# A decoder layer on one core: splits of the first pair's DMA sums queued behind the input's turned half, turns two ahead of products, first logistic functions at the end

## The chip, the core and the metric

The kernel runs on one core of one Trainium2 chip. The time is the device time of one execution in microseconds (us). TensorE (PE in the profile) does the matrix products, PEld its weight loads, VectorE (DVE) and ScalarE (ACT) the elementwise work, GpSimd (POOL) elementwise work and the issue of summing DMAs, SyncE (SP) the issue of the other DMAs.

## What is computed

One inference step of a hybrid decoder layer: a prompt of 1024 rows and 64 sample rows (8 x 8), 1024 wide, go through a root-mean-square norm, one wide input projection (seven slices of 512 columns and three gates of 1024), three branches and a gated merge.

```
def layer(x, ...):
    h = rmsnorm(x, g_pre)
    proj = h @ w_in                        # 1024 x (7*512 + 3*1024)
    p_in, p_gate, c_val, c_glu, c_gate, q, x_gate = slices of 512
    a     = pool_mix(p_in) * silu(p_gate)
    u     = c_val * sigmoid(c_glu)         # then depthwise conv 31, layernorm, silu
    bconv = conv_branch(u) * silu(c_gate)
    cattn = attention(q, mem_kv(mem)) * silu(x_gate)
    merged = sum over 3 of sigmoid(merge_logits) * (branch @ w_branch)
    return x + rmsnorm(merged @ w_out, g_post)
```

## The kernel before, in words

Everything is float32 outside; a product is made of float16 halves. `hilo` (line 74) splits a tile: ScalarE writes the high half (line 75), VectorE or, where asked, GpSimd the rest (lines 77 and 79). `mm3` (line 81) makes one product of three matmuls (lines 85, 88, 89): high by high, high by low, low by high.

The input projection goes by pairs of 128 output columns. `pair` (line 446) makes a 2 x 2 block product with seven products instead of eight: the left factors are blocks of the weight and their sums s1 to s4, the right ones are blocks of the turned (transposed) input, B11, B21, B22, and differences T1 to T4. The input's factors are made once, at the start, and kept in `BO`; those of the weight are made for every pair. The weight's sums are DMAs that add into the loaded tile: ScalarE negates two blocks (line 498), GpSimd issues the four sums one after the other (lines 499, 505, 506, 507), each after the landing of the one before. Then the sums are split as the other blocks are. The first `pair` of the list (the value half of the convolution's gate) is begun early: its product of a11 and of a12 are made in the start (`early`).

`startup` (line 236) is a generator. It norms and turns the first half of the input (512 rows: B11, B21), makes the first product with it for two blocks of gate columns (`first`, tiles `sg0`), takes the logistic function of each with its eviction (line 280), then turns the second half. `second_half(k)` (line 290), for k from 0 to 3, turns two blocks, each into a PSUM bank of the kind pb (4 banks), and makes of them by VectorE (lines 292 and 295) two differences `tq`, and by `hilo` the block B12, the block B22 and T1. T2 to T4 follow from `tq`: T3 and T4 are differences that GpSimd makes (lines 312 and 313), T4's low half too. The second half of the gate columns is then made with B12 and B22, and the sample rows (`BS`) follow. `mem_kv` (line 336) scales the 256 memory rows, whose norm's root was begun in the start (line 272).

The program is written in one order, but a scheduler that simulates the timeline places the instructions of each engine; each engine then runs its queue in order. Program order sets who is preferred: in the start the first product of the second gate block stands between `second_half(0)` and `second_half(1)`, and the splits of the pair's sums (lines 475 to 478, tiles `ws`) may go anywhere that their data allow.

Of the kernel before, what the change touches and what calls it, by code (L numbers as in the profile page):

```python
# [9 lines left out]
ALU = mybir.AluOpType  # L11
# [35 lines left out]
def hybrid_layer_kernel(ctx, tc, i, o):  # L47
# [23 lines left out]
    def tiny(shape, dt=F32):  # L71
        return sb.tile(shape, dt, tag="tiny", bufs=24, name=nm("t"))
# [80 lines left out]
        nc.vector.scalar_tensor_tensor(r, r, sc, t, ALU.mult, ALU.mult)  # L153
        return r

    def rstd_of(ss, inv_n, sc=1.0):
        p, n = ss.shape
        s = tiny([P, n])[:p]
        nc.scalar.activation(s, ss, AF.Sqrt, scale=inv_n, bias=eps[:p])
        v = tiny([P, n])[:p]  # L160
        nc.vector.tensor_scalar(v, ss, inv_n, EPS, ALU.mult, ALU.add)
        return newton(s, v, (p, n), sc)
# [3 lines left out]
        (eng or nc.sync).dma_start(out=x[:rows], in_=src)  # L166
        return x[:rows]

    def rstds(xs):
        ss = tiny([P, len(xs)])[: xs[0].shape[0]]  # L170
        for t, x in enumerate(xs):
            nc.scalar.activation(junk[: x.shape[0]], x, AF.Square, accum_out=ss[:, t : t + 1])
        return rstd_of(ss, 1.0 / D)

    BO = cst.tile([P, 7, 2, 4, HALF], F16, name="BO")
    junk = BO[:, 6].rearrange("p a k n -> p (a k n)")[:, : 2 * D].bitcast(F32)
# [59 lines left out]
    def startup():  # L236
# [32 lines left out]
                rs_.append(rstds(xt[k + 1 - k // 4 * 2 : k + 3 - k // 4 * 2]))  # L269

        xs_r = rstds([xs])
        mem["r"] = rstds(mems)
        sg0.update({r: Q([P, T]) for r in range(2)})

        def first(r, t0, ops):
            p = pm()
            for kh in range(2):
                w, n = w0[2 * kh + r], ops[kh]
                mm3(p, [(w[:, 0, k, :], w[:, 1, k, :], n(k)[0], n(k)[1]) for k in range(4)], kh == 0, kh == 1)
            nc.scalar.activation(sg0[r][:, t0 : t0 + HALF], p, AF.Sigmoid, scale=1.0 / WS)  # L280

        first(0, 0, [lambda k: bo(B11, k), lambda k: bo(B21, k)])
        scale_x(xt[4:6], rs_[0], True)
# [6 lines left out]
        def second_half(k):  # L290
            p, gk = flip(k, 1)
            nc.vector.scalar_tensor_tensor(tq[k][:, 0], p, gk, hx[k][:, 0], ALU.mult, ALU.subtract)
            hilo(p, b12[k // 2][:, 0, k % 2], b12[k // 2][:, 1, k % 2], gk)
            p, gk = flip(k + 4, 1)
            nc.vector.scalar_tensor_tensor(tq[k][:, 1], p, gk, tq[k][:, 0], ALU.mult, ALU.subtract)
            hilo(p, *bo(B22, k), gk)
            hilo(tq[k][:, 0], *bo(T1, k), -1.0)

        second_half(0)
        yield  # L300
        first(1, 0, [lambda k: bo(B11, k), lambda k: bo(B21, k)])
        yield
        for k in range(1, 4):
            second_half(k)
            yield
        for k in range(4):
            hilo(tq[k][:, 1], *bo(T2, k), -1.0)
        for r in range(2):
# [19 lines left out]
        for r in range(2):  # L328
            for kh in range(2):
                w = w0[2 * kh + r]  # L330
                mm3(p[:, r * NS : (r + 1) * NS], [(w[:, 0, k, :], w[:, 1, k, :], BS[:, 0, 4 * kh + k, :], BS[:, 1, 4 * kh + k, :]) for k in range(4)], kh == 0, kh == 1)
            nc.scalar.activation(sg0[r][:, S:], p[:, r * NS : (r + 1) * NS], AF.Sigmoid, scale=1.0 / WS)

    def mem_kv():
        memT = [Q([P, 2, KT // 2, NMEM], F16) for _ in range(2)]
        for t, m in enumerate(mems):
            nc.vector.tensor_scalar(m, m, mem["r"][:, t : t + 1], None, ALU.mult)

# [62 lines left out]
    def states():  # L403
        stc = Q([120, 2, W])
        nc.sync.dma_start(
            out=stc, in_=i["state_conv"][0].rearrange("b r c -> (b r) c").rearrange("(a p) c -> p a c", p=120))
        stp = Q([120, W])
        nc.sync.dma_start(out=stp, in_=i["state_pool"][0].rearrange("b r c -> (b r) c"))
        pwr = Q([P, WT, P])
        nc.sync.dma_start(out=pwr, in_=i["pool_w"][0].rearrange("g c d -> c g d"))  # L410
        yield
        for ch in range(WT):
            p = pb()
            for a in range(2):
                nc.tensor.transpose(p[:, a * 120 : (a + 1) * 120], stc[:, a, ch * P : (ch + 1) * P], ident[:120, :120])
            nc.scalar.activation(us[:, ch, :, :CB], p[:, :240].rearrange("p (b j) -> p b j", b=DB), AF.Copy)
            if ch % 2:
                yield
        p = pb()
        for g in range(WT):  # L420
            nc.tensor.transpose(p[:, g * 120 : (g + 1) * 120], stp[:, g * P : (g + 1) * P], ident[:120, :120])
        nc.scalar.activation(es[:, :, :, :PB], p[:, :480].rearrange("p (g b j) -> p g b j", g=WT, b=DB), AF.Copy)
        nc.gpsimd.memset(corr, 1.0)
        for g, win in enumerate(WINS):
            for j in range(win - 1):
                nc.gpsimd.memset(corr[:, g, j : j + 1], float(win) / (j + 1))
        hilo(pwr, pws[:, 0], pws[:, 1], WS)
        yield
        nc.sync.dma_start(out=o["conv_s"][0][:, : CB - DS, :], in_=i["state_conv"][0][:, DS:, :])
        nc.sync.dma_start(out=o["pool_s"][0][:, : PB - DS, :], in_=i["state_pool"][0][:, DS:, :])  # L430
        yield
# [14 lines left out]
    def pair(c0, dest, block, smp, sc=1.0 / WS):  # L446
# [26 lines left out]
                prep_a11()  # L473

        def prep1():
            spl("s1", lambda: v["s1"])
        def prep2():
            spl("s2", lambda: v["s2"])
        def prep3():
            spl("a12", lambda: A(0, 1))  # L480

# [930 lines left out]
```

## Time and profile before

| | us |
|---|---|
| median of 3 runs | 921.75 (921.71 to 926.39) |
| profiled execution | 925.56 |
| its span, first to last instruction | 923.8 |
| mean granted clock of TensorE | 0.965 |
| busy: PE / DVE / ACT / POOL | 859.6 / 715.1 / 465.2 / 360.3 |

A row of a timeline gives the start, the duration, the engine, the line, the operation and its tiles (out<-in, buffer numbers left out), the count of like instructions merged in the row, and in brackets the idle time of the engine ahead of it and what ended it. A row of stages gives start:end, the length, the busy time of each engine with its count of instructions, the granted clock of TensorE (1.00 is full), the share of DMA and GB/s. A row of groups gives count, busy us, mean ns, and idle time before.

### The profile page before, as it was taken

How to read it: one execution, taken by the hardware profiler on the slowest of the kernel's cores; microseconds unless marked ns; L12 is line 12 of the kernel's file. 1: busy time of each engine (PE TensorE's matmuls, PEld its weight loads, DVE VectorE, ACT ScalarE, POOL GpSimd, SP SyncE). 2: the span in 40 equal slices, each digit the busy share in tenths (PEclk: the TensorE clock that was granted, in tenths of full speed). 3: DMA queues.
4: the chain of work that ended last, by engine and by line, in shares of the span. 5: the costliest groups of instructions: out<-in, count | busy, mean ns of one | idle time of the engine just before them, and what ended most of it. 6: DMA issues, size and time to landing. Idle time of an engine off the chain costs nothing.

```text
span 923.8 us, 15244 instructions
## 1 busy us (share of the span) xinstructions
PE 859.6 (93%) x5765; PEld 461.0 (50%) x5765; DVE 715.1 (77%) x1119; ACT 465.2 (50%) x990; POOL 360.3 (39%) x392
## 2 busy tenths in 40 slices
PE   5879999999999889999998989999999999988986
PEld 3325455554555545555444445565545555545432
DVE  4697599999967699999988978458565544678876
ACT  8766547554753733323444544356345434745541
POOL 1354152444343361311443775525355212366500
PEclk8869999999999899999999999999999999998998
DMA  8634742424466224334444336444654658472132
GB/s 300 158 65 144 210 97 56 82 68 113 106 224 176 92 39 102 82 80 92 93 95 92 80 86 123 113 110 97 139 117 105 138 122 251 101 158 60 69 126 91
DMA packets 101541, 107.43 MB, mean 116 GB/s; under 512 B 5486, under 2 KB 72036, under 8 KB 101452
## 3 DMA queue, kind: packets, MB, share of 16 engines
q1 hardware_dynamic: 82748, 68.24, 23.5%
q0 software_dynamic: 18720, 38.22, 23.1%
q8 instruction: 45, 0.74, 0.3%
q14 instruction: 28, 0.23, 0.1%
HBM read 62.37 MB, written 6.33 MB: 74 GB/s over the span
## 4 chain that ended last, share of the span: by engine, by line
PE 37%; DVE 15%; issue 5%; ACT 3%; POOL 3%; DMA 3%; DVEq 0%; ACTq 0%; POOLq 0%
PE pm L85 8%; PE pm L89 8%; PE pm L88 8%; DVE q L715 6%; PE pb L85 4%; PE pb L89 4%; PE pb L88 4%; DVE ws L79 3%; DMA raw<-raw 2%; DVE ws L77 1%; POOL sr L594 1%; ACT ws L75 1%; DVE q L1272 1%; DVE q L1265 1%; DVE q L1155 1%
## 5 line engine op out<-in xcount | busy, mean ns | idle before, releaser
L85 PE MATMUL pm<-BO,ws 128*128 128x512 f16 x836 | 319.9, 385 | 17.8 <-ACT h L513 3.7
L89 PE MATMUL pm<-BO,ws 128*128 128x512 f16 x836 | 320.8, 384 | 3.1 <-DVE ws L77 2.8
L88 PE MATMUL pm<-BO,ws 128*128 128x512 f16 x836 | 321.1, 384 | 1.1 <-DVE BO L77 0.6
L79 DVE SCALAR_TENSOR_TENSOR ws<-raw,ws 128x512 f16<-128x512 f32 x228 | 192.9, 863 | 61.2 <-ACT ws L75 59.5
L88 PEld LDWEIGHTS <-ws 128*128 128x128 f16 x1548 | 149.1, 99 | 134.8 <-issue 27.7
L89 PEld LDWEIGHTS <-ws 128*128 128x128 f16 x1548 | 149.3, 99 | 125.0 <-issue 8.0
L85 PEld LDWEIGHTS <-ws 128*128 128x128 f16 x1548 | 148.7, 99 | 117.7 <-issue 9.5
L75 ACT ACTIVATE ws<-raw 128x512 f16<-128x512 f32 x228 | 138.1, 627 | 119.5 <-PE pm L89 57.0
L715 DVE SCALAR_TENSOR_TENSOR q<-q,cw,q 128x1024 f32<-128x1024 f32 x120 | 166.9, 1399 | 4.3 <-ACT q L712 4.0
L85 PE MATMUL pb<-q,ws 128*128 128x364 f16 (+1 forms) x288 | 92.2, 323 | 2.1 <-DVE q L1155 2.1
L89 PE MATMUL pb<-q,ws 128*128 128x364 f16 (+1 forms) x288 | 93.0, 323 | 0.0
L88 PE MATMUL pb<-q,ws 128*128 128x364 f16 (+1 forms) x288 | 92.9, 323 | 0.0
L499 POOL DMA_DIRECT2D raw<-raw x25 | 21.8, 872 | 150.3 <-ACT raw L498 134.1
L513 ACT ACTIVATE h<-pm 128x512 f32<-128x512 f32 x75 | 44.0, 588 | 50.8 <-PE pm L89 47.2
L1155 DVE SCALAR_TENSOR_TENSOR q<-pb,q 128x364 f32<-128x364 f32 (+1 forms) x72 | 37.1, 528 | 30.0 <-PE pb L89 24.4
L466 DVE SCALAR_TENSOR_TENSOR q<-pm,h 128x512 f32<-128x512 f32 x51 | 34.9, 684 | 21.3 <-PE pm L89 13.3
L507 POOL DMA_DIRECT2D raw<-raw x25 | 22.1, 885 | 68.5 <-issue 24.3
L75 ACT ACTIVATE q<-q 128x1024 f16<-128x1024 f32 (+2 forms) x37 | 35.5, 971 | 26.5 <-DVE q L867 12.6
L506 POOL DMA_DIRECT2D raw<-raw x25 | 21.6, 864 | 64.6 <-DVE ws L79 24.7
L498 ACT ACTIVATE raw<-raw 128x512 f32<-128x512 f32 x50 | 31.0, 626 | 30.7 <-DVE ws L79 29.9
L85 PE MATMUL pm<-BS,ws 128*128 128x64 f16 x416 | 43.3, 193 | 1.2 <-DVE q L466 1.2
L664 ACT ACTIVATE q<-q 128x512 f32<-128x512 f32 x36 | 22.6, 627 | 41.7 <-DVE q L466 41.2
(245 smaller groups left out, 1335.1 us busy)
## 6 DMA issues: line engine op xcount, KB each, us to landing
raw<-in_w_in SPq DMA_DIRECT2D x104, 256.0 KB, 2.9
raw<-raw POOLq DMA_DIRECT2D x104, 256.0 KB, 3.2
q<-in_x_prompt SPq DMA_DIRECT2D x16, 512.0 KB, 9.1
q<-q POOLq DMA_DIRECT2D x14, 544.0 KB, 5.5
raw<-in_w_branch SPq DMA_DIRECT2D x24, 256.0 KB, 3.9
q<-in_w_mem_kv SPq DMA_DIRECT2D x8, 512.0 KB, 6.7
q<-in_cache_mem_k SPq DMA_DIRECT2D x8, 512.0 KB, 3.4
q<-in_cache_mem_v SPq DMA_DIRECT2D x8, 512.0 KB, 7.3
```

Of the source, the lines that this page charges most:

```text
L75: nc.scalar.activation(hi, src, AF.Copy, scale=scale)
L79: nc.vector.scalar_tensor_tensor(lo, src, scale, hi, ALU.mult, ALU.subtract)
L85: ins = nc.tensor.matmul(out, wh, xh, start=start and j == 0, stop=False, skip_group_check=partial)
L88: nc.tensor.matmul(out, wh, xl, start=False, stop=False, skip_group_check=partial)
L89: nc.tensor.matmul(out, wl, xh, start=False, stop=stop and j == n - 1, skip_group_check=partial)
L466: nc.vector.scalar_tensor_tensor(dst, ps, sc, base, ALU.mult, ALU.add)
L498: nc.scalar.activation(A(1, kh), A(1, kh), AF.Copy, scale=-1.0)
L507: nc.gpsimd.dma_start(out=A(0, 1), in_=A(0, 0), accum_op=ALU.add)
L513: nc.scalar.activation(v[name], ps, AF.Copy, scale=sc)
L664: nc.scalar.activation(dst, src, AF.Sigmoid, scale=scale)
L715: ins = nc.vector.scalar_tensor_tensor(acc, src, wj, acc, ALU.mult, ALU.add)
L1155: nc.vector.scalar_tensor_tensor(g, p, 1.0 / WS, g, ALU.mult, ALU.mult)
```

## The change

- The splits of s1 and s2 of the first pair, the end of the memory rows' norm and the split of the pooling weight are put in the queues of ScalarE and VectorE behind the last split of T1 (`second_half(3)`), by `queued()`. The scheduler may not place them ahead of it.
- `second_half(1)` now stands ahead of the second gate block's first product, and `second_half(2)` right behind it.
- The logistic function is no longer taken with each eviction of `sg0`: these are copies now, and at the end of the start one logistic function over each whole tile (1088 columns) follows.
- The memory rows' squares and root stay in the start; the reciprocal root is made in `mem_kv`.

```diff
+    behind = []
+    def queued():
+        es_ = contextlib.ExitStack()
+        for ins in behind:
+            es_.enter_context(tc.issue_after(ins.ins))
+        return es_
...
-        mem["r"] = rstds(mems)
+        mem["ss"] = squares(mems)
+        mem["s"] = root_of(mem["ss"], 1.0 / D)
...
-            nc.scalar.activation(sg0[r][:, t0 : t0 + HALF], p, AF.Sigmoid, scale=1.0 / WS)
+            nc.scalar.activation(sg0[r][:, t0 : t0 + HALF], p, AF.Copy, scale=1.0 / WS)
...
-            hilo(tq[k][:, 0], *bo(T1, k), -1.0)
+            hi, lo = bo(T1, k)
+            a = nc.scalar.activation(hi, tq[k][:, 0], AF.Copy, scale=-1.0)
+            return a, nc.vector.scalar_tensor_tensor(lo, tq[k][:, 0], -1.0, hi, ALU.mult, ALU.subtract)
         second_half(0)
         yield
+        second_half(1)
+        yield
         first(1, 0, [lambda k: bo(B11, k), lambda k: bo(B21, k)])
+        second_half(2)
         yield
-        for k in range(1, 4):
-            second_half(k)
-            yield
+        behind.extend(second_half(3))
+        yield
...
-            nc.scalar.activation(sg0[r][:, S:], p[:, r * NS : (r + 1) * NS], AF.Sigmoid, scale=1.0 / WS)
+            nc.scalar.activation(sg0[r][:, S:], p[:, r * NS : (r + 1) * NS], AF.Copy, scale=1.0 / WS)
+            nc.scalar.activation(sg0[r], sg0[r], AF.Sigmoid)
...
     def mem_kv():
+        with queued():
+            mem["r"] = rstd_of(mem["ss"], 1.0 / D, s=mem["s"])
...
-        hilo(pwr, pws[:, 0], pws[:, 1], WS)
+        with queued():
+            hilo(pwr, pws[:, 0], pws[:, 1], WS)
...
         def prep1():
-            spl("s1", lambda: v["s1"])
+            with queued() if ahead else contextlib.nullcontext():
+                spl("s1", lambda: v["s1"])
         def prep2():
-            spl("s2", lambda: v["s2"])
+            with queued() if ahead else contextlib.nullcontext():
+                spl("s2", lambda: v["s2"])
```

How the queues change is read from the instructions of each engine in their new order. The lines of the changed file are some other lines: L77, L79 and L81 there are L75, L77 and L79 of before, L301 and L313, L316 are L280 and L292, L295, L319 and L320 the two halves of T1, L337 and L338 are L312 and L313, L530 to L538 are L499 to L507, L544 is L513, L161 and L169 are L159 and L161, L180 is L172.

ScalarE before, from the last square of the memory rows on (`raw_126` holds the first pair's s1, `raw_642` and `raw_645` the second pair's weights, `pb` a turned block, `q_328` a difference):

```order
L172 ACTIVATE BO,t_276<-q_106 128x1024
L75 ACTIVATE ws_648<-raw_126 128x512
L75 ACTIVATE ws_651<-raw_642 128x512
L75 ACTIVATE ws_654<-raw_645 128x512
L280 ACT_TABLE_LOAD
L280 ACTIVATE q_290<-pm_292 128x512
L159 ACT_TABLE_LOAD
L159 ACTIVATE t_279<-t_276,eps 128x2
L498 ACTIVATE raw_642<-raw_642 128x512
L498 ACTIVATE raw_645<-raw_645 128x512
L75 ACTIVATE q_326<-pb_332,g_pre 128x512
L75 ACTIVATE BO<-q_328 128x512
```

The same place in the changed kernel (`pb_323` is block 0's first turn, `pb_341` block 1's, `h_489` a difference that GpSimd makes):

```order
L180 ACTIVATE BO,t_276<-q_106 128x1024
L301 ACTIVATE q_281<-pm_283 128x512
L161 ACTIVATE t_279<-t_276,eps 128x2
L544 ACTIVATE h_375<-pm_362 128x512
L77 ACTIVATE q_317<-pb_323,g_pre 128x512
L319 ACTIVATE BO<-q_319 128x512
L77 ACTIVATE BO<-pb_331,g_pre 128x512
L77 ACTIVATE BO<-q_319 128x512
L77 ACTIVATE q_317<-pb_341,g_pre 128x512
L319 ACTIVATE BO<-q_320 128x512
L77 ACTIVATE BO<-h_489 128x512
L301 ACTIVATE q_282<-pm_377 128x512
```

The three splits, the table loads and the two negations are gone from here; the turned half follows the square at four steps' distance, and the copy of the bank `pm_377` stands behind the split of `h_489`.

GpSimd before, from the first pair's first sum on (`raw_123` and `raw_126` are the first pair's, `raw_642` and `raw_645` the second's):

```order
L499 DMA raw_126<-raw_123 128x512
L505 DMA raw_123<-raw_123 128x512
L506 DMA raw_123<-raw_126 128x512
L499 DMA raw_645<-raw_642 128x512
L507 DMA raw_126<-raw_123 128x512
L312 TENSOR_TENSOR h_498<-q_328,q_136 128x512
L313 TENSOR_TENSOR h_499<-q_136,q_328 128x512
L505 DMA raw_642<-raw_642 128x512
L506 DMA raw_642<-raw_645 128x512
```

GpSimd in the changed kernel, from the same sum on:

```order
L530 DMA raw_126<-raw_123 128x512
L536 DMA raw_123<-raw_123 128x512
L537 DMA raw_123<-raw_126 128x512
L337 TENSOR_TENSOR h_489<-q_319,q_136 128x512
L338 TENSOR_TENSOR h_490<-q_136,q_319 128x512
L538 DMA raw_126<-raw_123 128x512
L79 TENSOR_TENSOR BO<-h_490,BO 128x512
L337 TENSOR_TENSOR h_497<-q_320,q_137 128x512
L338 TENSOR_TENSOR h_498<-q_137,q_320 128x512
L79 TENSOR_TENSOR BO<-h_498,BO 128x512
```

Block 0's differences now stand ahead of the fourth sum but still behind the third; the second pair's sums have left this place, and come after the last block's differences.

VectorE in the changed kernel, from the low half of the last T1 on (`ws` are the splits of weights, `pb_445` is the last turned block):

```order
L320 SCALAR_TENSOR_TENSOR BO<-q_322,BO 128x512
L169 TENSOR_SCALAR t_673<-t_276 128x2
L147 RECIPROCAL t_675<-t_279 128x2
L81 SCALAR_TENSOR_TENSOR ws_641<-raw_126,ws_641 128x512
L1379 COPY parT<-pb_614 128x24
L1385 COPY cw<-pb_614 128x31x4
L81 SCALAR_TENSOR_TENSOR ws_644<-raw_635,ws_644 128x512
L81 SCALAR_TENSOR_TENSOR ws_647<-raw_638,ws_647 128x512
L81 SCALAR_TENSOR_TENSOR ws_653<-raw_123,ws_653 128x512
L81 SCALAR_TENSOR_TENSOR ws_656<-raw_635,ws_656 128x512
L152 TENSOR_TENSOR t_677<-t_675 128x2
L81 SCALAR_TENSOR_TENSOR BO<-pb_445,g_pre,BO 128x512
```

All five splits of weights stand here now, three of which (of `raw_126`, `raw_642`, `raw_645` in the names of before) stood ahead of the turned half.

More of the change, by code (lines that the diff above doesn't have):

```diff
@@ L2 @@
+import contextlib
 import concourse.bass as bass
@@ L154, in newton, with root_of @@
         return r
-    def rstd_of(ss, inv_n, sc=1.0):
+    def root_of(ss, inv_n):
         p, n = ss.shape
@@ L159, in rstd_of @@
         nc.scalar.activation(s, ss, AF.Sqrt, scale=inv_n, bias=eps[:p])
+        return s
+    def rstd_of(ss, inv_n, sc=1.0, s=None):
+        p, n = ss.shape
+        if s is None:
+            s = root_of(ss, inv_n)
         v = tiny([P, n])[:p]
@@ L167, in load, with squares @@
         return x[:rows]
-    def rstds(xs):
+    def squares(xs):
         ss = tiny([P, len(xs)])[: xs[0].shape[0]]
@@ L172, in rstds @@
             nc.scalar.activation(junk[: x.shape[0]], x, AF.Square, accum_out=ss[:, t : t + 1])
-        return rstd_of(ss, 1.0 / D)
+        return ss
+    def rstds(xs):
+        return rstd_of(squares(xs), 1.0 / D)
+    behind = []
[4 more added lines that the diff above has]
+        return es_
     BO = cst.tile([P, 7, 2, 4, HALF], F16, name="BO")
```

## The prediction

> **What bounds the kernel now.** I read the page first, for the share of TensorE (PE); then busy time by stage over the start; then the timelines of ScalarE (ACT), VectorE (DVE), GpSimd (POOL) and TensorE between 30 and 82 us. On the page, PE is near 9 tenths nearly everywhere but at both ends, so what the start loses is not hidden later.
>
> ```profile
> span 923.8 us, 15244 instructions
> PE   5879999999999889999998989999999999988986
> ```
>
> Busy time by stage (start:end, length, then busy us and instructions of PE, PEld, DVE, ACT, POOL, then the granted clock):
>
> ```profile
> 40.50:44.70 4.20, 0.02 (x1) 0.00 (x0) 1.56 (x4) 4.16 (x8) 1.11 (x2) 0.90 0.45 81
> 44.70:54.00 9.30, 6.88 (x19) 2.87 (x19) 9.24 (x13) 8.49 (x15) 4.81 (x5) 0.50 0.68 139
> 54.00:60.80 6.80, 3.21 (x17) 1.46 (x15) 6.80 (x8) 1.72 (x3) 4.92 (x4) 0.99 0.21 39
> 60.80:71.00 10.20, 9.22 (x28) 3.60 (x28) 10.20 (x13) 6.84 (x12) 6.66 (x5) 0.51 0.00 1
> 80.00:100.00 20.00, 20.00 (x163) 10.96 (x161) 16.98 (x27) 14.48 (x27) 6.13 (x9) 1.00 0.78 224
> ```
>
> From 40.5 to 44.7 TensorE does nothing; until 71.0 it is thinly fed and runs at half clock twice; from 80 it is full at clock 1.00. So the stage from 34 to about 80 us is where the change has to pay. What ACT and DVE wait for there:
>
> ```profile
> 37.93 1.67 ACT L75 ACTIVATE ws<-raw 128x512 f16<-128x512 f32 x3 [3.83 <-DMA raw<-raw]
> 39.61 1.28 ACT L280 ACT_TABLE_LOAD   x1
> 41.52 1.28 ACT L159 ACT_TABLE_LOAD   x1
> 44.06 0.67 ACT L75 ACTIVATE q<-pb,g_pre 128x512 f16<-128x512 f32 x1
> 45.26 1.28 ACT L280 ACT_TABLE_LOAD   x1
> ```
> ```profile
> 34.38 0.15 DVE L161 TENSOR_SCALAR t<-t 128x2 f32<-128x2 f32 x1
> 38.59 1.90 DVE L79 SCALAR_TENSOR_TENSOR ws<-raw,ws 128x512 f16<-128x512 f32 x3 [4.05 <-ACT ws L75]
> 40.40 0.74 DVE L292 SCALAR_TENSOR_TENSOR q<-pb,g_pre,q 128x512 f32<-128x512 f32 x1
> 43.14 0.17 DVE L145 RECIPROCAL t<-t 128x2 f32<-128x2 f32 x1 [2.00 <-ACT t L159]
> 44.76 0.75 DVE L79 SCALAR_TENSOR_TENSOR q<-pb,g_pre,q 128x512 f16<-128x512 f32 x1 [0.70 <-ACT q L75]
> ```
>
> ACT stands for 3.83 us before three splits, the first of which needs a sum that a DMA makes; DVE stands behind the same splits for 4.05 us, then 2.00 us behind ACT's two table loads and square root, then 0.70 us. Only at 44.06 does ACT take the high half of the input's first turned block, although DVE had nothing to do from 34.53 (34.38 + 0.15). The sums are issued by GpSimd, whose queue is in order too:
>
> ```profile
> 32.19 1.01 POOL L499 DMA_DIRECT2D raw<-raw  x1 [5.45 <-DMA raw<-in_w_in]
> 38.21 0.86 POOL L505 DMA_DIRECT2D raw<-raw  x1 [5.01 <-DMA raw<-raw]
> 41.97 0.86 POOL L506 DMA_DIRECT2D raw<-raw  x1 [2.90 <-DMA raw<-raw]
> 46.25 1.59 POOL L312 TENSOR_TENSOR h<-q,q 128x512 f32<-128x512 f32 x1
> 47.48 1.58 POOL L313 TENSOR_TENSOR h<-q,q 128x512 f32<-128x512 f32 x1
> ```
>
> **The change, part by part.** *The splits move behind the turned half.* In the new order VectorE's first subtraction of block 0 comes where VectorE ran dry at 34.53, and its transposes stand ahead of the last 29 products that TensorE did before 40.5, so they are there; I start it at 34.6 instead of 40.40. The waits of 4.05, 2.00 and 0.70 us go. The five splits that stood among this work (three at 38.59, two more later) come back behind it, at five times the SBUF price below. Unit prices, start to start, from three rows:
>
> ```profile
> 61.99 0.73 DVE L79 SCALAR_TENSOR_TENSOR q<-pb,g_pre,q 128x512 f16<-128x512 f32 x1
> 62.65 0.67 DVE L79 SCALAR_TENSOR_TENSOR BO<-q,BO 128x512 f16<-128x512 f32 x1
> 63.24 0.68 DVE L77 TENSOR_TENSOR BO<-h,BO 128x512 f16<-128x512 f32 x1
> ```
>
> A step that reads PSUM takes 0.66 us, one that reads SBUF only 0.59 us.
>
> *VectorE's new path.* Ten steps come first (seven from PSUM, three from SBUF): 7 x 0.66 + 3 x 0.59 = 6.4 us, so 41.0. The eleventh is the low half of block 0's first difference, and that difference is GpSimd's. GpSimd is where something new is late: its difference stands behind the third sum, whose issue waited for a landing until 41.97. With that issue 0.86, the difference 1.23 (46.25 to 47.48) and ACT's half 0.67, VectorE goes on at 44.7: a new wait of 3.7 us. In the kernel before, the differences also stood behind the sums, but nobody was ready for them.
>
> The fourth sum comes between block 0's differences and block 1's. Issue to landing was 41.97 - 38.21 = 3.76 us, so it issues at 45.7; then 0.86, two GpSimd steps of 1.23 and ACT's 0.67 give 49.7 for the low half of block 1's difference. VectorE has four steps until there (2.5 us, to 47.2) and loses about 1.7 to GpSimd in them (next paragraph); that leaves a second wait of 0.8 us.
>
> From 44.7 to the low half of the sample rows (the last thing TensorE needs before the product of T1) are 15 steps from SBUF, 10 from PSUM and 0.6 us of small ones: 8.9 + 6.6 + 0.6 = 16.1 us. This counts the five splits; the two scalings of the memory rows and most of their small steps now stand behind it.
>
> *What GpSimd takes from VectorE.* In this stage VectorE's steps from SBUF are stretched whenever GpSimd works, those from PSUM are not. Groups of DVE from 38 to 77 us (count, busy us, mean ns):
>
> ```profile
> L79 DVE SCALAR_TENSOR_TENSOR BO<-q,BO 128x512 f16<-128x512 f32 x8 | 9.1, 1139 | 0.0
> L77 DVE TENSOR_TENSOR BO<-h,BO 128x512 f16<-128x512 f32 x4 | 5.2, 1288 | 0.0
> L152 DVE TENSOR_SCALAR t<-t 128x2 f32<-128x2 f32 x1 | 3.0, 3006 | 0.0
> L79 DVE SCALAR_TENSOR_TENSOR pws<-q,pws 128x512 f16<-128x512 f32 x1 | 1.8, 1750 | 0.0
> ```
>
> Against 0.67 us undisturbed: 8 x 0.47 + 4 x 0.62 + 2.86 (a step of 0.15) + 1.08 = 10.2 us for 12 GpSimd steps. All twelve are still there; the first now falls into VectorE's own wait, so 11/12, 9.3 us. The 2.86 is one accident in which two GpSimd steps passed ahead of one tiny step; without it the term is 6.4, and if the waiting is worse for the new neighbours I bound it by the old 10.2. I take 9.3, since the same steps meet. VectorE is done at 44.7 + 16.1 + 0.8 + 9.3 = 70.9.
>
> *TensorE.* The rows of before at the end of the stage:
>
> ```profile
> 76.39 1.04 PE L353 MATMUL pb<-ident,q 128*128 128x128 f32 x8
> 77.26 0.38 PE L88 MATMUL pm<-BO,ws 128*128 128x512 f16 x1
> 77.69 0.58 PE L415 MATMUL pb<-ident,q 120*128 120x120 f32 x4
> 78.10 0.19 PE L85 MATMUL pm<-BS,ws 128*128 128x64 f16 x1
> 78.80 0.38 PE L85 MATMUL pm<-BO,ws 128*128 128x512 f16 x1
> 81.39 1.04 PE L353 MATMUL pb<-ident,q 128*128 128x128 f32 x8
> ```
>
> The product of T1 runs from 78.80 to 81.39: 12 matmuls at 0.216 us. The 24 small ones of the sample rows take 0.70 us ahead of it. Before them stand 12 transposes (0.87 + 0.41 us) which the new order has behind the product; so the same point is 81.39 - 1.28 = 80.1 before. After: 70.9 + 0.70 + 2.59 = 74.2. Is TensorE itself later than 70.9? Block 2's halves are there at about 55 (44.7, four SBUF and seven PSUM steps, a third of the stretch); 38 products follow until the sample rows, 8.2 us at full clock, 16.3 at half. At full clock till 60.8 and half after, as in the rows above, they end at 66: hidden behind VectorE. Gain 80.1 - 74.2 = **5.9 us**.
>
> *Edits that I cost at nothing.* Two of the three table loads go with the two early logistic functions (2.56 us of ACT); VectorE's next waits are for GpSimd, and hide it. The logistic at the end is one load and two ACT steps over 1088 columns (about 1.2 us each, at the 1.67 us for 3 x 512 above), behind the stage; what needs it first is the gating of the first pair's outputs, GpSimd's, which also waits for the memory rows' splits ahead of it on VectorE. The second pair's sums stood among block 0's and block 1's steps on GpSimd and now come after block 3's differences, near 66; the first product with one of them stands more than 36 products after T1 (8 us), at 82 or later, and a sum lands in 3.8 to 5.7 us: hidden, with about 10 us to spare. The scaling of the memory rows moves behind the stage, to about 72; its transposes come after T1, at 74.2: hidden by 2 us, and costing up to those 2 us if VectorE is later. The next weights' load waits for the buffer that the s3 split frees, and moves forward with it.
>
> *Carry.* From 80 us TensorE is full, so 5.9 us arrive at the end unless a later stage gives some back. The profiled execution took 925.56 us (span 923.8 and 1.8 around it), the median is 921.75; a difference worked out in the one is taken off the other: 921.75 - 5.9 = **915.9 us**.
>
> **A rule against it.** At 40.5, where it ran empty before, TensorE now has four products and eight transposes, 1.7 us (0.216, and 0.87/8), and then waits for a PSUM bank that ACT copies only behind block 0's difference, at about 45.3: a gap of 3.1 us. In the rows, half clock came for 9 to 10 us after the empty stage at 40.5, and again at 60.8 after gaps of which the longest was this:
>
> ```profile
> 58.61 0.59 PE L85 MATMUL pm<-q,ws 128*128 128x512 f16 x2 [2.04 <-ACT q L75]
> ```
>
> So 2.04 us sufficed, with TensorE 3.21 of 6.80 us busy. The Trainium skill ("TensorE: Matmul & The Clock Gate", Part 1) gives half rate after an idle window of about 3.4 us and full rate after a busy one, the windows running freely. By that rule a gap of 3.1 us would mostly leave the clock full, and the sum stays 74.2; half clock to the end would have next to no chance. The second half-clock stage here speaks against so clean a rule; I go by the rows and give that case 0.10.
>
> **The rivals.** *Half clock to the end of the stage* (slower). If the thin feeding from 45 to 57 keeps the clock at half until past T1: 38 products from 55 end at 71.3, the sample rows take 1.4, T1 5.2: 77.9, which is 3.7 later than 74.2; then the next 12 large and 48 small products at half rate cost 4.0 us more. That is 7.7 us lost of 5.9 gained, 1.8 us slower than before: 923.6. It decides from 27 products at half rate beyond the forecast (5.9/0.216). For it: both half-clock stages above. Against: after 54.0 the clock was back at 0.99 though TensorE was 6.88 of 9.30 us busy.
>
> *The sums land late.* The first took 37.93 - 32.19 = 5.7 us, the second 3.76. If the second and third take 5.7, the first difference is 2.0 us later, and the fourth sum holds block 1's difference until 53.7 instead of 49.7: 4.0 us in all, so 1.9 us gained, 919.9. Against: the second was already 3.76 while weights still came in.
>
> *A later stage gives some back.* The new order has one half of a weight load (line 195) behind two stores of the pooling tails where it stood ahead of them:
>
> ```profile
> 496.37 14.25 SPq L195 DMA_DIRECT2D raw<-in_w_in  x4
> 513.65 0.61 SPq L749 DMA_DIRECT2D out_pool_s<-h  x1
> 517.80 1.36 ACT L498 ACTIVATE raw<-raw 128x512 f32<-128x512 f32 x2 [2.21 <-DVE ws L79]
> 521.04 0.87 POOL L499 DMA_DIRECT2D raw<-raw  x1
> ```
>
> The four pieces of the load were all issued by 496.37 + 14.25 = 510.6; behind the stores the last half goes out at 514.3, some 3.6 us later. Its sum is issued at 521.04, 1.9 us after ACT's negation ended, so 1.7 of the 3.6 show, and all 3.6 if GpSimd gets there earlier: 917.6 to 919.5, say 918.5. Small exchanges on VectorE between 100 and 450 us could do as much in either direction.
>
> *More.* If the accident of 2.86 us doesn't come again: 8.8 us, 913.0.
>
> **How the numbers follow.** Forecast 0.50, more 0.08, later give-back 0.17, late sums 0.15, half clock 0.10. A measurement of this kernel can tell about 0.5%, 4.6 us. Faster by more than that (below 917.1): the forecast but for 0.04 of it, "more", and 0.02 from the others: 0.56. Slower by more: 0.07, from half clock with worse feeding than worked out, and later exchanges. Within: 0.37. The range runs from 911, with the stretch also down to half (4.7), to 921.5, which holds the late sums and the give-back and leaves out most of half clock.
>
> **What would show it.** In the changed profile: ACT without a wait near 34 to 38 us and the first turned half on ACT near 35.5 (step 1); no table load between 34 and 70; VectorE idle about 3.7 us near 41, released through ACT from GpSimd, with GpSimd's third sum at 42 ahead of it (the new wait); GpSimd's next sums after 60; T1's product done near 74; TensorE full from then on. The forecast is wrong if the wait at 41 is absent or over 6 us, if the granted clock is half after 71, or if the gain at T1 is there and the end doesn't show it.

## The result, and the profile after

| | before | changed |
|---|---|---|
| median of 15 runs each, us | 923.49 (921.71 to 927.08) | 919.19 (913.17 to 921.14) |
| profiled execution, us (span) | 925.56 (923.8) | 921.1 (919.3) |
| mean granted clock | 0.965 | 0.968 |

The ratio is 0.9942, with a 95% interval of 0.9924 to 0.9959: 0.6% faster, about 5.4 us. Two later measurements of the same kernel gave 0.9933 (0.9909 to 0.9957) and 0.9945 (0.9927 to 0.9963).

The page's head, then busy time by stage (start:end, length, busy us of PE, PEld, DVE, ACT, POOL, granted clock):

```profile
span 919.3 us, 15244 instructions
PE   5979999899999879899999989999999999988986
```
```profile
40.50:44.70 4.20, 4.20 (x24) 2.38 (x23) 4.20 (x4) 1.85 (x4) 3.75 (x4) 1.00 0.34 62
44.70:54.00 9.30, 4.29 (x22) 2.12 (x21) 9.30 (x12) 4.69 (x10) 5.55 (x5) 0.85 0.33 83
54.00:60.80 6.80, 6.80 (x23) 2.79 (x22) 6.80 (x10) 6.80 (x14) 4.58 (x4) 0.50 0.00 1
60.80:71.00 10.20, 9.13 (x65) 4.70 (x64) 10.13 (x18) 5.61 (x12) 6.63 (x6) 0.97 0.15 27
80.00:100.00 20.00, 19.61 (x116) 9.19 (x113) 15.32 (x22) 13.22 (x24) 5.78 (x9) 1.00 0.77 214
```

TensorE works through 40.5 to 44.7, where it stood before, and is at half clock once (54 to 60.8) instead of twice. VectorE is busy through 40.5 to 60.8 and for 10.13 of the 10.20 us behind: it is the bound of this stage now. Its rows from the first subtraction of the turned half to the sample rows' low half:

```profile
36.60 0.75 DVE L313 SCALAR_TENSOR_TENSOR q<-pb,g_pre,q 128x512 f32<-128x512 f32 x1 [2.14 <-PE pb L248]
...
41.37 3.41 DVE L81 SCALAR_TENSOR_TENSOR BO<-q,BO 128x512 f16<-128x512 f32 x1
45.36 1.60 DVE L320 SCALAR_TENSOR_TENSOR BO<-q,BO 128x512 f16<-128x512 f32 x1
46.88 1.75 DVE L79 TENSOR_TENSOR BO<-h,BO 128x512 f16<-128x512 f32 x1
49.21 1.31 DVE L81 SCALAR_TENSOR_TENSOR BO<-q,BO 128x512 f16<-128x512 f32 x1
...
58.42 1.23 DVE L169 TENSOR_SCALAR t<-t 128x2 f32<-128x2 f32 x1
59.64 1.76 DVE L81 SCALAR_TENSOR_TENSOR ws<-raw,ws 128x512 f16<-128x512 f32 x1
61.63 4.22 DVE L81 SCALAR_TENSOR_TENSOR ws<-raw,ws 128x512 f16<-128x512 f32 x4
67.10 1.12 DVE L1383 TENSOR_SCALAR psc<-parT 128x4 f32<-128x4 f32 x1
69.33 0.68 DVE L79 TENSOR_TENSOR BS<-h,BS 128x512 f16<-128x512 f32 x1
```

The first subtraction comes at 36.60 and not at 34.6; behind 36.60 there is no idle time in brackets, but long steps: eight rows here take 10.3 us more than at 0.67 us (0.60 for each further one in a row, 0.15 to 0.17 for the small steps). GpSimd and TensorE in the same stage:

```profile
37.08 0.86 POOL L536 DMA_DIRECT2D raw<-raw  x1 [3.89 <-DMA raw<-raw]
40.84 0.86 POOL L537 DMA_DIRECT2D raw<-raw  x1 [2.90 <-DVE q L316]
41.40 1.59 POOL L337 TENSOR_TENSOR h<-q,q 128x512 f32<-128x512 f32 x1
42.63 1.58 POOL L338 TENSOR_TENSOR h<-q,q 128x512 f32<-128x512 f32 x1
44.33 0.88 POOL L538 DMA_DIRECT2D raw<-raw  x1
```
```profile
49.43 0.63 PE L248 MATMUL pb<-ident,q 128*128 128x128 f32 x4 [2.28 <-DVE BO L81]
51.95 1.01 PE L87 MATMUL pm<-q,ws 128*128 128x512 f16 x2 [1.89 <-ACT q L77]
70.73 0.38 PE L87 MATMUL pm<-BO,ws 128*128 128x512 f16 x1
73.32 0.38 PE L381 MATMUL pb<-ident,q 128*128 128x128 f32 x2
```

The first difference still stands behind the third sum, as forecast, but no one waits for it: VectorE's long step from 41.37 covers the two differences (41.40 to 44.21). The product of T1 runs from 70.73 to 73.32; the same point was 80.11 before, so 6.8 us are won there.

### The profile page after: what moved, and what is told of

The parts are those of the page before. It is cut to its first block, busy times and chain, and to the rows that moved or that the text cites. A ratio compares the mean times of both kernels' runs of the same rounds, so it can differ in the third digit from the quotient of the medians.

```text
span 919.3 us, 15244 instructions
## 1 busy us (share of the span) xinstructions
PE 857.1 (93%) x5765; PEld 459.6 (50%) x5765; DVE 722.3 (79%) x1119; ACT 465.5 (51%) x990; POOL 357.3 (39%) x392
## 4 chain that ended last, share of the span: by engine, by line
PE 31%; DVE 8%; issue 5%; POOL 3%; DMA 2%; ACT 2%; DVEq 0%; POOLq 0%; ACTq 0%
PE pm L91 7%; PE pm L87 7%; PE pm L90 7%; PE pb L90 3%; PE pb L91 3%; PE pb L87 3%; DMA raw<-raw 2%; DVE ws L81 2%; DVE ws L79 1%; POOL sr L625 1%; DVE q L1303 1%; DVE q L1296 1%; DMA q<-q 1%; POOL raw L1248 1%; DVE q L79 0%
## 5 line engine op out<-in xcount | busy, mean ns | idle before, releaser
L81 DVE SCALAR_TENSOR_TENSOR ws<-raw,ws 128x512 f16<-128x512 f32 x228 | 198.7, 887 | 51.3 <-ACT ws L77 47.6
L77 ACT ACTIVATE ws<-raw 128x512 f16<-128x512 f32 x228 | 138.6, 626 | 120.6 <-PE pm L91 61.1
L530 POOL DMA_DIRECT2D raw<-raw x25 | 22.1, 883 | 158.7 <-ACT raw L529 142.6
L544 ACT ACTIVATE h<-pm 128x512 f32<-128x512 f32 x75 | 44.3, 592 | 55.5 <-PE pm L91 52.4
L77 ACT ACTIVATE q<-q 128x1024 f16<-128x1024 f32 (+2 forms) x37 | 35.6, 975 | 30.3 <-DVE q L898 14.7
L538 POOL DMA_DIRECT2D raw<-raw x25 | 21.9, 878 | 65.2 <-issue 20.7
L87 PE MATMUL pm<-BS,ws 128*128 128x64 f16 x416 | 43.5, 193 | 2.6 <-DVE q L495 2.6
L90 PE MATMUL pm<-BS,ws 128*128 128x64 f16 x416 | 43.4, 193 | 1.1 <-DVE BS L79 1.1
L91 PE MATMUL pm<-BS,ws 128*128 128x64 f16 x416 | 43.1, 193 | 0.0
```

Of the source, the lines that this page charges most:

```text
L77: nc.scalar.activation(hi, src, AF.Copy, scale=scale)
L81: nc.vector.scalar_tensor_tensor(lo, src, scale, hi, ALU.mult, ALU.subtract)
L87: ins = nc.tensor.matmul(out, wh, xh, start=start and j == 0, stop=False, skip_group_check=partial)
L90: nc.tensor.matmul(out, wh, xl, start=False, stop=False, skip_group_check=partial)
L91: nc.tensor.matmul(out, wl, xh, start=False, stop=stop and j == n - 1, skip_group_check=partial)
L530: nc.gpsimd.dma_start(out=A(1, 1), in_=A(1, 0), accum_op=ALU.add)
```

## The experiments

Two measures of where time goes are used beside the ratios. The first is the start of the row behind T1's twelve matmuls ("T1 done"); it moves by up to 1.3 us with the transposes that an order puts ahead. The second is free of the order: from all of TensorE's matmuls (those of zeros left out), the time by which as many moving columns were done, taken off the same time in the profiled execution before. I call it the lead. It is that of one execution: three of the changed kernel differ by up to 1.9 us in it. The profiled execution before was 2 us above its median, so a lead at the end is about 2 us more than the difference of the medians. (The expectation of the kernel with both edits quotes 11.3 and 2.9 us from a rougher count; they are 12.4 and 3.1.)

| kernel | median, us | ratio (95%) | T1 done | lead at 100 us | 440 | 500 | 880 |
|---|---|---|---|---|---|---|---|
| changed | 919.19 | 0.9942 (0.9924 to 0.9959) | 73.32 | 6.2 | -0.3 | 5.8 | 5.6 |
| changed, 2nd | 918.51 | 0.9933 (0.9909 to 0.9957) | 71.95 | 7.5 | 1.6 | 7.5 | 7.5 |
| changed, 3rd | 917.94 | 0.9945 (0.9927 to 0.9963) | 73.05 | 6.4 | 0.4 | 6.3 | 6.3 |
| sums free | 923.23 | 1.0008 (0.9989 to 1.0027) | 76.06 | 5.1 | 2.2 | 1.9 | 2.0 |
| turns back | 921.94 | 0.9981 (0.9962 to 1.0) | 75.54 | 5.8 | 4.2 | 4.7 | 3.9 |
| logistic back | 922.50 | 0.9997 (0.9978 to 1.0015) | 73.16 | 2.6 | -1.6 | 4.1 | 4.3 |
| queue alone | 923.00 | 0.9986 (0.9972 to 1.0) | 75.27 | 5.1 | 4.0 | 4.4 | 3.6 |
| ten more steps | 926.70 | 1.003 (1.0014 to 1.0045) | 83.35 | -2.0 | -3.4 | -3.5 | -3.6 |
| pauses filled | 915.67 | 0.9927 (0.9898 to 0.9956) | 70.37 | 9.1 | 2.4 | 8.2 | 7.8 |
| all on VectorE | 921.64 | 0.9964 (0.9945 to 0.9983) | 67.17 | 12.4 | 7.3 | 7.3 | 3.1 |
| filled and VectorE | 916.43 | 0.9922 (0.9893 to 0.9952) | 64.89 | 14.6 | 9.1 | 9.2 | 7.0 |
| filled, sums last | 916.05 | 0.9923 (0.9897 to 0.995) | 71.29 | 8.8 | 5.8 | 10.2 | 8.5 |

**One part undone at a time.** (The edits shift lines by a few in some kernels.) The sums' splits free again:

```diff
-        behind.extend(second_half(3))
+        second_half(3)
```

> The changed kernel with the splits of the first pair's sums, the memory rows' finishing steps and the pooling weights' split free again (nothing is queued behind the turned half); turns ahead of products and logistic functions at the end are kept. Theory (the queue holds the gain): VectorE gets five splits of 0.68 us and the small steps back in front of or among its turned steps, and the sums reach GpSimd ahead of its differences, so the T1 product is done at 77 to 80 us (73.32 in the changed kernel, 80.11 before) and the time is 922 to 924 us. Rival (the two turns ahead of the products hold it): the T1 product stays at 73 to 75 us and the time at 919 to 920.5 us.

The time is as the theory had it (923.23), the place only in part. T1 is done at 76.06, with about 1.3 us of transposes ahead of it, and at 100 us the lead is 5.1 us, where the changed kernel has 6.2 to 7.5. More is lost later: 2.3 us by 160 us, and the regain of about 6 us that the changed kernel has between 440 and 500 us is missing.

The turns in the order of before:

```diff
         second_half(0)
-        yield
-        second_half(1)
         yield
         first(1, 0, [lambda k: bo(B11, k), lambda k: bo(B21, k)])
+        yield
+        second_half(1)
+        yield
         second_half(2)
```

> The changed kernel with the program order of before for the turns (one turn, the second product, three turns); the queue and the logistic functions at the end are kept. Theory (VectorE runs without a pause from its first subtraction on, so that each microsecond at its start is one at the end): the second product's 24 matmuls lie ahead of the turns again, the first subtraction comes at 38.5 to 40.4 us instead of 36.60, the T1 product is done at 75 to 77 us, the time is 921 to 923 us. Rival (the second product's matmuls fill the two holes of 1.06 and 1.01 us that TensorE has at 21 and 25 us in the changed kernel, the clock is back at 26.5 instead of 30.7 us, and that pays for the order): the first subtraction at 36 to 37 us and the time within 1 us of 919.2.

The time (921.94) lies in the theory's range, but the start goes the rival's way: the first subtraction is at 34.41 us, earlier than in the changed kernel and than either expected. What then costs is a wait that the changed kernel doesn't have. VectorE is busy for 0.92 of the 4.20 us from 40.5 and waits 5.88 us in all, for the high half of a difference that GpSimd begins only at 45.01 us, behind the third and the fourth sum:

```profile
34.41 0.74 DVE L313 SCALAR_TENSOR_TENSOR q<-pb,g_pre,q 128x512 f32<-128x512 f32 x1
47.30 1.08 DVE L79 TENSOR_TENSOR BO<-h,BO 128x512 f16<-128x512 f32 x1 [5.88 <-ACT BO L77]
```
```profile
40.50:44.70 4.20, 3.62 (x22) 2.01 (x19) 0.92 (x2) 0.00 (x0) 1.11 (x2) 1.00 0.34 62
```

The logistic functions back at the evictions:

```diff
-            nc.scalar.activation(sg0[r][:, t0 : t0 + HALF], p, AF.Copy, scale=1.0 / WS)
+            nc.scalar.activation(sg0[r][:, t0 : t0 + HALF], p, AF.Sigmoid, scale=1.0 / WS)
...
-            nc.scalar.activation(sg0[r][:, S:], p[:, r * NS : (r + 1) * NS], AF.Copy, scale=1.0 / WS)
-            nc.scalar.activation(sg0[r], sg0[r], AF.Sigmoid)
+            nc.scalar.activation(sg0[r][:, S:], p[:, r * NS : (r + 1) * NS], AF.Sigmoid, scale=1.0 / WS)
```

> The changed kernel with the logistic functions back at the three evictions of each tile, and so with ScalarE's table loads of before; all else is kept. Theory (edits at nothing): VectorE sets the pace, three table loads of 1.28 us on ScalarE are covered, the T1 product stays within 0.7 us of 73.32 and the time within 1 us of 919.2. Rival (ScalarE's high halves hold VectorE's low halves, so the loads in front of them count): the T1 product 2.5 to 4 us later, the time 921.5 to 923 us.

Up to T1 the theory holds to 0.2 us (73.16): the table loads are covered. The time follows the rival all the same. A loss stands behind T1: the scheduler put twelve matmuls of a product elsewhere, and TensorE then waited for a bank that ScalarE empties, so that 2.6 us of lead are left at 100 us. First this kernel, then the changed one:

```profile
83.19 0.59 PE L87 MATMUL pm<-BO,ws 128*128 128x512 f16 x1 [2.54 <-ACT h L543]
```
```profile
83.80 0.38 PE L87 MATMUL pm<-BO,ws 128*128 128x512 f16 x1 [0.39 <-ACT h L544]
```

But the profiled execution was the fastest of the twelve (919.86 us), and at 880 us its lead of 4.3 is only 1.3 below the changed kernel's 5.6. Where the median loses the rest the trace doesn't show.

**The queue alone**, with the last two edits together:

> The changed kernel with the order of turns and products of before and the logistic functions back at the evictions: of the change only what is queued behind the turned half is left (and the memory rows' split finish). Theory (the parts need one another: the turns let VectorE start at once, the queue leaves it free, the logistic part settles the products' order at 80 us): 922 to 924 us, no gain that can be told from none. Rival (the queue is most of it): 919.5 to 921 us.

923.0 us: no gain that can be told from none. So the parts don't add. Each of the four partial kernels is 2.6 to 5.8 us ahead at 100 us, and each ends between the two kernels or at the old time.

**Two short pauses and the clock.** TensorE between 20 and 26 us, before and after:

```profile
20.80 0.63 PE L85 MATMUL pm<-BO,ws 128*128 128x512 f16 x1
24.57 0.63 PE L88 MATMUL pm<-BO,ws 128*128 128x512 f16 x1
```
```profile
22.05 0.58 PE L90 MATMUL pm<-BO,ws 128*128 128x512 f16 x1 [1.06 <-DVE BO L79]
25.77 0.59 PE L90 MATMUL pm<-BO,ws 128*128 128x512 f16 x1 [1.01 <-DVE BO L79]
```

Before, matmuls of the second gate block filled the time in which the first one waited for low halves: the row at 20.80 shortened the first wait (0.63 us were left), the rows up to 24.57 and on left none of the second. In the new order the turns are preferred, which aren't ready; those matmuls come later, and TensorE pauses for 1.06 and 1.01 us. The granted clock in the same microseconds, the changed kernel first, then its second measurement:

```profile
25.00:26.00 1.00, 0.23 (x1) 0.10 (x1) 1.00 (x2) 0.04 (x1) 1.00 (x2) 0.50 1.07 327
30.00:31.00 1.00, 1.00 (x5) 0.39 (x4) 1.00 (x3) 0.47 (x1) 0.00 (x0) 0.65 1.15 344
```
```profile
25.00:26.00 1.00, 0.14 (x1) 0.00 (x0) 1.00 (x1) 0.29 (x1) 1.00 (x2) 0.82 1.33 413
30.00:31.00 1.00, 1.00 (x7) 0.43 (x5) 1.00 (x4) 0.09 (x1) 0.00 (x0) 1.00 1.01 292
```

In one execution the clock is back at 25.4 us, in the other at 30.7 (0.65 = half until then, full from there), with the same pauses. The pauses filled with matmuls of zeros (`nil`, three behind the first matmul of k = 0 and of k = 2 in the first product), which leave 0.70 us of the first pause and 0.29 of the second:

```diff
+                    if (r, t0, kh) == (0, 0, 0) and k in (0, 2):
+                        for _ in range(3):
+                            nc.tensor.matmul(p, nil, xh, start=False, stop=False)
```

> The changed kernel with six more matmuls of a weight tile of zeros, three in each of the two places in the first product where TensorE waited 1.06 and 1.01 us for a low half (they add zero to the same bank). Theory (those two short pauses kept TensorE at half clock until 30.7 us, 4.2 us longer than in the kernel before, and that made the turned half 2 us late): the granted clock is full from 26 to 27.5 us, VectorE's first subtraction at 34.4 to 35.2 us, the T1 product 1.5 to 2 us earlier than 73.32, the time 917 to 918 us. Rival A (the clock doesn't hang on these pauses): half clock to 30.7 us, first subtraction at 36.6, the time 919.2 us. Rival B (clock and subtraction come as said, but the sums on GpSimd's queue then stand in VectorE's way, as was forecast): T1 product at 73 us and the time 919 us.

The subtraction came as the theory said (34.49 us). The clock was back sooner than it said (24.8 us), T1 was 2.95 us earlier and the time 915.67 us, both better than it said. The changed kernel again:

> The changed kernel itself, unaltered, beside the runs of this call: all theories expect the ratio of its first measurement, 0.994 of before (919.2 us). A ratio of 0.998 or more would say that the first 15 runs were lucky and that the three kernels with one part undone (0.998 to 1.001) hardly differ from it.

> The changed kernel itself once more, beside the two below on their chip: a ratio of 0.992 to 0.996 of before. Its profiled run tells more of its start: in two profiled runs TensorE paused alike (1.06 and 1.0 us at 21 and 25 us), and the clock was back at 26 us in one and at 30.9 us in the other. Theory (pauses only give the clock a chance to come back late): either of the two again, and the first subtraction at 34.5 to 35.5 us or at 36.4 to 37.4 us accordingly.

The ratios were 0.9933 and 0.9945. The clock was back at 25.4 and 29.8 us and the first subtraction came at 35.49 and 36.05 us, with 30.7 at 36.60: the later the clock, the later the subtraction, though 36.05 lies just below the range expected.

Over the 13 profiled executions: without the two pauses of 1 us (before, turns back, queue alone and the three filled kernels) the clock was back between 24.8 and 26.8 us in six of six; with them between 29.8 and 31.8 in six of seven and at 25.4 in one. So the pauses don't set the time of the return, but seem to decide whether an early one is missed. The Trainium skill ("TensorE: Matmul & The Clock Gate", Part 1) says that the clock is judged over windows of about 3.4 us that run freely, so that one kernel warms up at different points; the two executions above agree with that. It also asks for an idle window before the clock drops; here it fell at 51.2 us, within the second of two pauses (2.28 and 1.89 us, the rows at 49.43 and 51.95 above) with four transposes between them: TensorE was busy for 0.63 of the 3.41 us before the drop.

**VectorE is the bound.** Ten subtractions done twice or three times:

```diff
-            nc.vector.scalar_tensor_tensor(tq[k][:, 0], p, gk, hx[k][:, 0], ALU.mult, ALU.subtract)
+            for _ in range(3 if k < 2 else 2):
+                nc.vector.scalar_tensor_tensor(tq[k][:, 0], p, gk, hx[k][:, 0], ALU.mult, ALU.subtract)
...
-            nc.vector.scalar_tensor_tensor(tq[k][:, 1], p, gk, tq[k][:, 0], ALU.mult, ALU.subtract)
+            for _ in range(2):
+                nc.vector.scalar_tensor_tensor(tq[k][:, 1], p, gk, tq[k][:, 0], ALU.mult, ALU.subtract)
```

> The changed kernel with ten of VectorE's subtractions of the turned half done again (the same values are written, nothing else is altered): 10 x 0.66 us more on the engine that has no pause between 36.6 and 71 us. Theory (VectorE sets the end of the startup, and what is won there is carried): the T1 product is done at 79 to 80.5 us, as in the kernel before (80.11), and the time goes back to that of before, 922.5 to 926 us. Rival (a later stage takes back what the startup wins or loses): the T1 product is as late, the time no more than 921 us. Rival B (VectorE has room): the T1 product at 73 to 76 us.

926.7 us, 8.2 us more than the changed kernel measured beside it (918.51), for 6.6 us of steps; T1 is done 10 us later (83.35). Both are more than the theory had. VectorE has little room to hide the steps, but not all of T1's 10 us is its own: its last low half ahead of T1 ends 4.2 us later (74.83 for 70.62), not 6.6, as it is held less (5.4 us for 10.5). The rest is TensorE's: the memory rows' transposes stand ahead of T1 here and wait 0.74 us for VectorE, and, fed more thinly, it was at half clock from 74.8 to 81.8 us.

```profile
71.00:80.00 9.00, 5.57 (x41) 4.21 (x41) 7.21 (x15) 4.28 (x10) 3.01 (x3) 0.70 0.49 89
```

**GpSimd's steps hold VectorE's.** All twelve done by VectorE:

```diff
-                nc.gpsimd.tensor_tensor(t3, tq[k][:, 1], hx[k][:, 0], ALU.subtract)
-                nc.gpsimd.tensor_tensor(t4, hx[k][:, 1], tq[k][:, 1], ALU.subtract)
+                nc.vector.tensor_tensor(t3, tq[k][:, 1], hx[k][:, 0], ALU.subtract)
+                nc.vector.tensor_tensor(t4, hx[k][:, 1], tq[k][:, 1], ALU.subtract)
...
-                hilo(t4, *bo(T4, k), eng=nc.gpsimd)
+                hilo(t4, *bo(T4, k))
```

> The changed kernel with GpSimd's eight differences and four low halves of the startup done by VectorE: 12 steps of about 0.61 to 0.68 us more on VectorE (7.3 to 8.2 us), none on GpSimd, whose queue is left to the sums. Theory (VectorE's steps from SBUF are held while GpSimd works: between 41 and 68 us their stretches in the changed kernel sum to 10.6 us, 3.41 for 0.67 the longest): the T1 product 2 to 3.5 us earlier than 73.32 and the time 916 to 918 us. Rival (VectorE's long steps have another cause, or its added steps stand in line): the T1 product 4 to 8 us later, the time 923 to 927 us.

T1 is done 6.2 us earlier (67.17 against 73.32), with more to do on VectorE. Of the twelve steps nine stand ahead of the sample rows' low half, and one older step has gone behind it: 8 x 0.60 = 4.8 us more. From the first subtraction to the end of that low half VectorE takes 27.5 us instead of 33.4. So 5.9 + 4.8 = 10.7 us of hold are gone, which is what the rows say (10.3 us in eight of them, 0.4 in a ninth at 53.68): the hold is shown. But the time misses the theory's range: only 2.2 us of the median are won on before, less than in the changed kernel. Of 12.4 us of lead at 100 us, 3.1 are left at 880. With the pauses filled as well:

> The changed kernel with both edits: TensorE's two pauses filled with matmuls of zeros, and GpSimd's twelve steps of the startup on VectorE. Theory (each removes a hold of its own): the clock is back by 27 us, the T1 product done at 65.5 to 66.5 us (67.8 with VectorE's steps alone, 70.4 with the filling alone). Of the time two theories speak: if what is won in the startup is carried as in the changed kernel, 910 to 913 us; if the later stages take it back, as they did with VectorE's steps alone (11.3 us ahead of the kernel before at 100 us, 2.9 us at 880), 917 to 921 us.

T1 is done at 64.89 us, earlier than expected, and the lead at 100 us is 14.6; 7.0 are left at 880, and the time of 916.43 us lies just below the second theory's range. One place where the two kernels lose 3.4 and 3.5 us (500 to 560 us) shows how a part of it goes. GpSimd, VectorE and TensorE of this kernel:

```profile
526.25 7.29 POOL L1030 TENSOR_TENSOR q<-q 128x1036 f32<-128x1036 f32 x3
```
```profile
525.87 5.46 DVE L81 SCALAR_TENSOR_TENSOR ws<-raw,ws 128x512 f16<-128x512 f32 x2 [0.89 <-ACT ws L77]
```
```profile
531.99 0.58 PE L87 MATMUL pm<-BO,ws 128*128 128x512 f16 x1 [5.31 <-DVE q L504]
```

Three sums of the pooling branch on GpSimd meet two splits on VectorE, which take 5.46 us instead of 1.3, and TensorE waits 5.31 us for the step behind them. The kernel before waits 3.21 us there, the changed one 1.97 and 1.36. The same hold, in another place: I read it as an earlier start that moves the meetings; where the rest of the lead goes was not followed.

**The wait that was forecast.** Where the transposes are early, it is there. The pauses filled:

```profile
41.07 1.59 POOL L346 TENSOR_TENSOR h<-q,q 128x512 f32<-128x512 f32 x1
```
```profile
43.36 1.09 DVE L79 TENSOR_TENSOR BO<-h,BO 128x512 f16<-128x512 f32 x1 [2.16 <-ACT BO L77]
45.16 0.75 DVE L81 SCALAR_TENSOR_TENSOR BO<-pb,g_pre,BO 128x512 f16<-128x512 f32 x1 [0.72 <-ACT BO L77]
48.45 1.07 DVE L79 TENSOR_TENSOR BO<-h,BO 128x512 f16<-128x512 f32 x1 [1.16 <-ACT BO L77]
```

VectorE waits 2.16 and 1.16 us for high halves of differences behind the third and fourth sum, and 0.72 us for the high half of a turned block, which ScalarE makes behind one of those. In the last kernel these two sums stand behind the first two blocks' differences:

```diff
+            with tc.issue_after(diffs[1].ins) if ahead else contextlib.nullcontext():
-            nc.gpsimd.dma_start(out=A(0, 0), in_=A(1, 1), accum_op=ALU.add)
-            nc.gpsimd.dma_start(out=A(0, 1), in_=A(0, 0), accum_op=ALU.add)
+                nc.gpsimd.dma_start(out=A(0, 0), in_=A(1, 1), accum_op=ALU.add)
+                nc.gpsimd.dma_start(out=A(0, 1), in_=A(0, 0), accum_op=ALU.add)
```

> The changed kernel with the two pauses filled, and the first pair's third and fourth sums queued on GpSimd behind the differences of the first two blocks. Theory (the wait that was forecast: with the transposes there at 34.5 us VectorE waited 2.16, 0.72 and 1.16 us for high halves of differences that stood behind the third and fourth sum, issued at 40.5 and 44.0 us): the first difference starts at 37.3 to 38.5 instead of 41.07 us, most of the 4.0 us of waits go, the T1 product is done at 66.5 to 69 us instead of 70.4, the time 912 to 915 us. Rival A (GpSimd's steps, now earlier, hold VectorE's steps from SBUF instead): the T1 product at 69.5 to 71.5 us, the time 915 to 917.5 us. Rival B (the sums, now later, are what the splits wait for): the splits after 62 us, the T1 product later than 71.5 us.

The waits are gone and rival A took their place: GpSimd's steps, earlier, hold VectorE's. T1 is done at 71.29 us, the time is 916.05.

```profile
38.62 1.59 POOL L346 TENSOR_TENSOR h<-q,q 128x512 f32<-128x512 f32 x1
39.85 1.59 POOL L347 TENSOR_TENSOR h<-q,q 128x512 f32<-128x512 f32 x1
```
```profile
38.97 3.02 DVE L81 SCALAR_TENSOR_TENSOR BO<-q,BO 128x512 f16<-128x512 f32 x1
42.58 1.31 DVE L329 SCALAR_TENSOR_TENSOR BO<-q,BO 128x512 f16<-128x512 f32 x1
43.82 1.75 DVE L79 TENSOR_TENSOR BO<-h,BO 128x512 f16<-128x512 f32 x1
```

The three kernels with filled pauses are the fastest measured (ratios 0.9922 to 0.9927); against the changed kernel measured beside them (917.94 us) the last two are 1.5 and 1.9 us faster, which the intervals don't tell from nothing.

## Why the prediction was right, and where it was not

The forecast was 915.9 us, the measured median 919.19. The gain was put at 5.9 us and came out as 4.3 by the medians, 5.4 by the ratio; the other 1.7 us of the difference is the median of before, which was 921.75 in three runs and 923.49 in fifteen. The step by step sum is another matter: two of its terms failed in opposite directions. By the prediction's own sign ("The forecast is wrong if the wait at 41 is absent") its account of VectorE's path is wrong, for that wait was absent. That the sum came so near is in part luck.

- **"Its transposes stand ahead of the last 29 products ..., so they are there" failed.** The first subtraction came 2.0 us late (36.60), since TensorE was at half clock until 30.7 us. I had looked for what the turns pass, not for what the second product's matmuls did where they stood: they kept TensorE busy. The filled kernels show it (34.08 to 34.49), and the second measurement, with the same pauses and the clock back at 25.4 us, came between (35.49).
- **"A new wait of 3.7 us" and the second of 0.8 us did not come** in the changed kernel. The mechanism was right: with the transposes early, the waits are 2.16 + 0.72 + 1.16 = 4.0 us in the filled kernel, and 5.88 us in the one with the turns back. In the changed one VectorE was 2.0 us later, the third sum 1.1 us earlier (40.84 for 41.97), and a held step filled the rest.
- **The hold by GpSimd** was 10.3 us in the eight rows for the forecast 9.3. From these: 36.6 + 6.4 + 16.1 + 10.3 = 69.4 for VectorE's end, measured 69.33 + 0.68 = 70.0, forecast 70.9. The step that failed is to add the waits to a hold of its own size. A wait and a hold take each other's place here: from the first subtraction to the sample rows' low half, VectorE's idle time plus what its steps took beyond 0.68 us (0.75 with an operand in PSUM, less for the small ones) sums to 0.1 + 10.5 us in the changed kernel, 4.2 + 5.4 in the filled one, 6.2 + 5.4 with the turns back, 4.0 + 7.5 with the queue alone and 0.1 + 10.9 with the sums last. The forecast had 4.5 + 9.3, too much by 3.2 us, and a start too early by 2.0. In the filled kernel, where the start and the waits are about as forecast, VectorE's end is at 67.1 and not at 70.9.
- **T1 done** at 73.3 for the forecast 74.2; 6.8 us won there for 5.9. The second pair's sums (from 65.61 us) and the memory rows' scaling (71.12 us) were hidden as costed.
- **The logistic functions, costed at nothing,** cost nothing up to T1, and in all, when put back, 3.3 us by the medians and 5.1 by the ratios. A wait of 2.54 us behind 80 us, from another order of products, is what the trace shows of it; the rest is open. Such an effect of a re-sorted order was not in the sum.
- **Half clock to the end** did not come: half from 51.2 to 61.4 us, full from there to 100 us. The rule of the Trainium skill that was weighed ("TensorE: Matmul & The Clock Gate", Part 1) gave it next to no chance, and the trace agrees; but the drop at 51.2 us itself came without the idle window that the rule asks for.
- **Carry.** "5.9 us arrive unless a later stage gives some back" is right in its result (6.2 us at 100 us, 5.6 at 880) and not in its way. The lead shrinks to -0.3 us at 440 us and comes back by 500, where the prediction allowed for no more than "small exchanges on VectorE". TensorE's busy time there, before and after:

```profile
440.00:500.00 60.00, 53.18 (x372) 26.80 (x369) 53.57 (x66) 28.01 (x55) 26.96 (x28) 1.00 0.43 97
```
```profile
440.00:500.00 60.00, 58.69 (x403) 29.39 (x402) 54.46 (x69) 29.27 (x57) 27.90 (x31) 1.00 0.47 103
```

The 5.5 us of TensorE's idle time that the changed order saves here are nearly as large as what it lost from 100 to 440 us (6.5). The rival's place, the weight load behind the pooling stores, cost nothing that shows: from 500 to 540 us, where its load went out behind the stores at 508.5, the lead was 5.8 and 6.1 us. Which change of order makes the loss and the regain was not isolated; that kernels with the old order of turns lose less by 440 us (5.8 to 4.2 and 5.1 to 4.0), and that these and the one with free splits (5.1 to 2.2) regain nothing worth the name by 500, only says that it comes with the order.

## What to carry to other kernels

A step that is moved takes with it what it did for others where it stood: look for the waits that it filled, and whether the clock was coming back in them. On an engine that another one holds, a wait and a hold are exchanged, so cost them together: taking the wait away won nothing, taking the other engine's work over won 6.2 us at T1 although 4.8 us more of steps stood ahead of it. And in a kernel that a scheduler orders, a gain at the start is a shift of all later meetings: of 3 to 15 us of lead at 100 us here, 2 to 9 reached the end, so measure a stage by its own end and the kernel by its time, and don't take the one for the other.

## What the runs showed of the hardware that was not expected

- TensorE's clock came back at 25.4, 29.8 and 30.7 us in three executions of one program with the same two pauses of 1.06 and 1.0 us. T1 came at 71.95, 73.05 and 73.32 us with them. The times (919.2, 917.6 and 921.1 us) don't follow: what of the spread of 913 to 921 us over the runs comes from this is open.
- VectorE's steps with two operands in SBUF are held through one or two whole steps of GpSimd: 3.41, 3.02, 1.75 us for 0.67; 5.46 for two splits. Small steps (128x2 and 128x4) are held too: 1.23 and 1.12 us for 0.15. Those with an operand in PSUM took 0.73 to 0.75 us beside the same GpSimd steps. The Trainium skill ("GPSIMD Engine Reference", 1. Specifications) says that GpSimd shares its SBUF interfaces with VectorE and that instructions with two SBUF inputs contend. The trace agrees, and gives the size: the GpSimd steps held VectorE for 10.7 us, more than the 12 x 0.60 = 7.2 us that it takes to do all twelve itself.
